# Loading the last DeltaNet pair into the gates' tile, and other banks and token orders for three blocks of an output projection

## The chip, the cores and the metric

The kernel runs on one core of a Trainium2 chip. The metric is the device time of one execution in microseconds. Engines are named as in the profile: PE is TensorE (matmuls; PEld its weight loads), DVE is VectorE, ACT is ScalarE, POOL is GpSimd, SP is SyncE, which here only issues DMAs. SPq, ACTq and POOLq are DMA issues on those engines' queues.

## The reference

One decoder layer for 512 tokens of width 2048, in fp32. Two causal token mixers work side by side on the normalised input, an mLSTM with 8 heads and a gated DeltaNet with 16 heads of 128 channels; their outputs go through one output projection each, are merged with sigmoid gates and added to the residual.

```python
u = _rmsnorm(h, norm_w)
proj = jnp.matmul(u, w_in)                    # 2048 x 20528, split into q, k, v, gates, ...
...
h_a = _mlstm_chunkwise(...)                   # then norm, sigmoid and silu gates
...
qkv = _causal_conv_silu(dn_qkv, dn_conv_w)    # four taps and silu on q, k, v of DeltaNet
...
h_b = _gated_delta_chunkwise(dq, dk_, dv_, beta, g)
h_b = _merge_heads(_rmsnorm(h_b, dn_norm_w)) * jax.nn.silu(dn_z)

y_a = jnp.matmul(h_a, w_out[:ML_WIDTH])
y_b = jnp.matmul(h_b, w_out[ML_WIDTH:])
return jax.nn.sigmoid(gate_a) * y_a + jax.nn.sigmoid(gate_b) * y_b
```

The result is `h + y`, and a last RMSNorm goes over it.

## The kernel before

Each fp32 operand of a big matmul is split into two parts of a faster format, hi and lo, and three products are added (hi x hi, hi x lo, lo x hi). For weights, `split_hi` is a cast on ACT (L135, `wh<-wr`) and `split_lo` a subtraction on DVE (L138, `wl<-wr,wh`). Weight tiles come through a ring: `wr` (raw, four buffers, loaded by SP), `wh` and `wl` (four buffers each). Of the activations, `uh` and `ul` are the two parts, made on ACT (L1189) and DVE (L1190) from raw tiles `hr`.

The kernel runs in stages. First come the input projections. Then DeltaNet heads are done in pairs (`dn_unit`; eight pairs, the last is pair 7 with heads 14 and 15), with the mLSTM heads beside them. Each `dn_unit` projects k, v and q of its pair into two PSUM banks, and `conv_silu` takes them out: a copy to `yp` on ACT (L770), a multiplication with the last tap on ACT (L771), three taps on DVE (L773). Behind the projections the mixers go on: a triangular solve on DVE (`xi`, L889 and L891), whose result travels over DRAM (`xd`, `tt`) and comes back as `tn` (L907), small matmuls, a chain per head that collects the output in a bank `po`, and at last `gz` (L1040), which empties that bank. The head's output is transposed and written to `h_d` by four DMAs on ACT's queue.

While the last pair's mixer is still at work, the output projection of the mLSTM branch begins: three *wide blocks* (`wide_block`) of 512 output columns, called blocks 0, 1 and 2. Each has 16 rows of weights (row k is `kt` = k), and for each row four token tiles of 128 tokens (token 0 to 3, `c` in the code), three matmuls of 512 columns each: 192 matmuls. The rows 14 and 15 (`KTAIL`) are done together at the end, token by token, and behind each token `put_y` multiplies the block's result with its gate tile (`tgy`, in block 2 a quarter of the tile `X`) and adds it to `y_d` in DRAM (L1338, L1339). Each token has a PSUM bank of its own, from one of three pools: `pj` (3 banks), `wk` (3) and `o` (2); the `po` of the two heads of a pair are the two `o` banks.

Behind block 2 comes `seven_stage`, a fast matrix scheme with seven products in place of eight, for the DeltaNet branch. It needs, for each of the eight pairs, sums and differences of the two heads' outputs in split form (`h_pair`: four sums on DVE, L1248 to L1251, the split `tu` on ACT and DVE, and a write of the changed raw tile to `he_d`), and all sixteen outputs as `uh` and `ul` (`load_h2`, which reads `he_d` and `h_d` into four buffers `hs`, tiles named `hr`). It also prepares its own weights: three tiles `wr3` at a time, their differences `t13` (L528, L529), split like the others and with the same rings. The profile leaves off the numbers at the end of a name, so it prints `wr3` as `wr` and `t13` as `t`.

These three, `h_last` (the pair 7), `load_h2` and the first weights of `seven_stage` (`lead`), run beside block 2. Their pool `sb` takes the room of the mixers' pool `wk`, so it opens only when the mixers' last tile there is free (`close`).

PE's order is that of the program: the generators that are started run at a `tick` between matmuls. The other engines' orders are set by a scheduler at build time, by priorities (`urgent(level)`) and dependencies (`behind`: no earlier than the newest split on that engine). Each engine, and each engine's DMA queue, then works strictly in its order.

Of the kernel before, what the change touches and what calls it, by code (L numbers as in the profile page):

```python
# [8 lines left out]
F32 = mybir.dt.float32  # L9
# [6 lines left out]
P = 128  # L16
S = 512
NC = S // P
D = 2048
KT = D // P  # L20
NB = 256
KP = 2
NO = 512
# [4 lines left out]
YDRAIN = 2  # L28
# [4 lines left out]
KTAIL = 2  # L33
# [22 lines left out]
def hybrid_body(  # L56
# [152 lines left out]
    def urgent(level=1):  # L209
        return tc.high_priority(offset=level * PRIO)  # L210
# [33 lines left out]
    psj = pss.enter_context(tc.tile_pool(name="psj", bufs=3, space=PSUM))  # L244
    psw = pss.enter_context(tc.tile_pool(name="psw", bufs=3, space=PSUM))
    pso = pss.enter_context(tc.tile_pool(name="pso", bufs=2, space=PSUM))

    banks = (((psj, "pj"),) * 3 + ((psw, "wk"),), ((psw, "wk"),) * 2 + ((pso, "o"),) * 2)

    def proj_cm(col0, before=None, kind="i"):  # L250
        ps = [psj.tile([P, S], F32, tag="pj", name="pj") for _ in range(2)]
# [511 lines left out]
    def bc(col, n):  # L763
        return col.unsqueeze(2).to_broadcast([P, NC, n])

    def conv_silu(ps, ct, dst, level=1):
        yp = yps[cnt["yp"] % NYP]
        cnt["yp"] += 1
        with urgent(level):
            A.copy(yp[:, 3:S + 3], ps)  # L770
            A.mul(dst, yp[:, 3:S + 3], convc[:, 144 + ct:145 + ct])  # L771
        for j in (2, 1, 0):
            V.scalar_tensor_tensor(out=dst, in0=yp[:, j:j + S], scalar=convc[:, 48 * j + ct:48 * j + ct + 1], in1=dst,  # L773
                                   op0=ALU.mult, op1=ALU.add)
# [268 lines left out]
    def dn_unit(p, mh):  # L1043
        hs = (2 * p, 2 * p + 1)
# [27 lines left out]
            start(load_h(), 2, "B")  # L1072
        ps = proj_cm(DN_Q + dcol)
        u["qn"] = []
        for j in range(2):
            conv_silu(ps[j], hs[j], kq[j][:, 1, :], 3 if last else 1)
            qn = wp.tile([P, NC, P], F32, tag="tg", name="qn", bufs=3)
            u["qn"].append(qn)
            start(silu_end(kq[j][:, 1, :], (kq[j][:, 1, :], qn)), 4 + 3 * j, front)
# [148 lines left out]

    def h_raw(i):
        if i == KH - 1:  # L1230
            raw = [late["sb"].tile([P, S], F32, tag="hs", name="hs", bufs=4) for _ in range(2)]
        elif i % 2:
            raw = [wk.tile([P, S], F32, tag="rb", name="hs", bufs=3) for _ in range(2)]
        else:
            pair = wk.tile([P, 2, S], F32, tag="ls", name="hs", bufs=1)
            raw = [pair[:, n, :] for n in range(2)]
        with behind("S"):
            for n in range(2):
                load_tile(raw[n], h_d[2 * i + n])
        return raw  # L1240
# [29 lines left out]

    def h_last():

        yield 5
        raw = h_raw(KH - 1)
        yield 5
        yield from h_pair(KH - 1, raw)
# [42 lines left out]
    def wide_w(col, kt):  # L1319
        return [w[:, 0, :] for w in next_w("o", col, kt)]  # L1320

    def wide_block(nb, pools, place, then=()):

        sl = slice(nb * NO, (nb + 1) * NO)
        ps = [pool.tile([P, NO], F32, tag=t, name="py") for pool, t in pools]
# [22 lines left out]
        for gen, wait in then:  # L1348
            start(gen, wait)
        ks = range(KT)  # L1350
        for kt in ks[:KT - KTAIL]:
            w = wide_w(nb * NO, kt)
            for c in range(NC):
                products(ps, kt, c, *w, ks)
                if c % 2:
                    tick()
            if nb < YDRAIN:
                close()
        ws = [(kt, wide_w(nb * NO, kt)) for kt in ks[KT - KTAIL:]]
        for c in range(NC):  # L1360
            for kt, w in ws:
                products(ps, kt, c, *w, ks)
            tick()
            if c in tgs:
                with urgent(3):
                    put_y(c)
            else:
                start(put_last(), 1)
# [2 lines left out]
             wk.tile([P, NO], F32, tag="rb", name="tgy", bufs=3) if c == 2 else wp.tile([P, NO], F32, tag="tg", name="tgy", bufs=3),  # L1371
             lambda c: wp.tile([P, NO], F32, tag="tg", name="tgy", bufs=3))
    for b in range(YDRAIN):
        wide_block(b, ((psj, "pj"), (psw, "wk"), (psj, "pj"), (psj, "pj")), DRAIN[b])
    while "sb" not in late:
        tick()
        close()
# [238 lines left out]
                    tick()  # L1616
            done_c(c)

    wide_block(YDRAIN, banks[1], lambda c: X2[:, c // 2, c % 2, :], [(load_h2(), 1), (lead(), 18)])
    for b, blk in enumerate(OUTS):  # L1620
        seven(2 * KH * b, *blk)
    last_block()
# [33 lines left out]
```

## Time and profile before

| | |
|---|---|
| median of 3 runs | 2229.91 us (2222.15 to 2234.51) |
| the profiled execution | 2228.3 us |
| its span in the profile | 2226.5 us |
| PE, DVE, ACT, POOL busy | 2157.8, 1650.0, 1022.2, 265.2 us |
| DMA, mean over the span | 196 GB/s |
| DMA from 1950 to 2010 us | 271 GB/s |

A timeline row has the start in us, the duration in us, the engine, the line of the kernel, the operation and `out<-in`, the number of rows merged into it (`x3`), and in brackets how long the engine was idle before it and what ended that. Matmuls are pipelined: a matmul's duration of 0.39 us is longer than the distance to the next one, so the time that a wait costs is read from the distance of the starts. Block 0 starts at 1846.95 us of the span, block 2 at 1951.2, `seven_stage` at 2005.69.

### The profile page before, as it was taken

The numbers are of one execution on the slowest core, as the hardware profiler recorded it, in microseconds if no ns is written. First come the engines' busy times: TensorE is split into PE (matmuls) and PEld (weight loads), VectorE is DVE, ScalarE is ACT, GpSimd is POOL, SyncE is SP. The second block draws the span as 40 slices with busy tenths as digits, with TensorE's granted clock in tenths as the row PEclk, the third lists the DMA queues.
The fourth block names the chain that finished last, engine by engine and source line by source line (L and its number), as shares of the span: only waits on it lengthen the run. The fifth ranks groups of instructions, "written<-read, shape, count | busy, mean of one in ns | idle before, by whom it ended". The sixth has DMA issues, their size and how long they took to land. (4 is left out here: it accounts for less than half of the span.)

```text
span 2226.5 us, 31649 instructions
## 1 busy us (share of the span) xinstructions
PE 2157.8 (97%) x10592; PEld 1770.6 (80%) x10592; DVE 1650.0 (74%) x2883; ACT 1022.2 (46%) x1986; POOL 265.2 (12%) x356
## 2 busy tenths in 40 slices
PE   6999999999999999999999999999999999989997
PEld 5877878888788788888888788888787887867775
DVE  5787788788778777877597786757575777567776
ACT  5444444445444444444545544444444454334344
POOL 0320000000000000000222412212122211110101
PEclk9999999999999999999999999999999999999999
DMA  5456666667667766776776767767666668695896
GB/s 156 124 176 197 196 202 198 209 200 234 192 211 232 236 197 215 231 241 190 198 201 165 172 161 174 165 160 172 161 145 162 152 157 230 176 268 184 247 323 220
DMA packets 534821, 435.81 MB, mean 196 GB/s; under 512 B 241921, under 2 KB 393698, under 8 KB 534530
## 3 DMA queue, kind: packets, MB, share of 16 engines
q1 hardware_dynamic: 425058, 357.68, 56.3%
q10 hardware_dynamic: 105568, 68.77, 9.7%
q0 software_dynamic: 4032, 7.34, 2.2%
q8 instruction: 83, 1.36, 0.2%
q14 instruction: 80, 0.66, 0.1%
HBM read 342.37 MB, written 95.49 MB: 197 GB/s over the span
## 5 line engine op out<-in xcount | busy, mean ns | idle before, releaser
L135 ACT CAST wh<-wr 128x512 fp32r<-128x512 f32 (+1 forms) x538 | 379.2, 706 | 416.3 <-PE pj L262 229.3
L138 DVE TENSOR_TENSOR wl<-wr,wh 128x512 fp32r<-128x512 f32 (+1 forms) x538 | 440.9, 822 | 152.9 <-ACT wh L135 142.7
L261 PE MATMUL pj<-uh,wh 128*128 128x512 f32 x1024 | 428.6, 419 | 0.0
L263 PE MATMUL pj<-uh,wl 128*128 128x512 f32 x1024 | 402.6, 393 | 0.0
L262 PE MATMUL pj<-ul,wh 128*128 128x512 f32 x1024 | 402.1, 393 | 0.0
L576 PE MATMUL ps<-wl,uh 128*128 128x512 f32 x704 | 277.7, 394 | 6.7 <-DVE wl L138 6.5
L575 PE MATMUL ps<-wh,uh 128*128 128x512 f32 x704 | 276.1, 392 | 6.3 <-DVE X L617 6.0
L577 PE MATMUL ps<-wh,ul 128*128 128x512 f32 x704 | 274.9, 391 | 0.0
L135 ACT CAST wh<-ts 128x512 fp32r<-128x512 f32 x224 | 138.2, 617 | 258.2 <-DVE ts L535 199.7
L135 ACT CAST wh<-t 128x1024 fp32r<-128x1024 f32 x112 | 117.8, 1052 | 250.0 <-PE ps L577 129.2
L263 PEld LDWEIGHTS pj<-uh,wl 128*128 128x128 f32 x1024 | 193.4, 189 | 42.6
L576 PE MATMUL ps<-wl,suh 128*128 128x512 f32 x576 | 224.3, 389 | 1.7 <-DVE wl L138 1.7
L575 PE MATMUL ps<-wh,suh 128*128 128x512 f32 x576 | 224.4, 390 | 0.6 <-ACT wh L135 0.3
L577 PE MATMUL ps<-wh,sul 128*128 128x512 f32 x576 | 224.1, 389 | 0.0
L261 PEld LDWEIGHTS pj<-uh,wh 128*128 128x128 f32 x1024 | 194.3, 190 | 35.2
L262 PEld LDWEIGHTS pj<-ul,wh 128*128 128x128 f32 x1024 | 194.3, 190 | 32.9
L138 DVE TENSOR_TENSOR wl<-ts,wh 128x512 fp32r<-128x512 f32 x224 | 153.7, 690 | 38.5 <-ACT wh L135 38.5
L138 DVE TENSOR_TENSOR wl<-t,wh 128x1024 fp32r<-128x1024 f32 x112 | 137.7, 1229 | 47.5 <-ACT wh L135 46.6
L576 PEld LDWEIGHTS ps<-wl,uh 128*128 128x128 f32 x704 | 132.3, 188 | 43.6 <-DVE wl L138 17.3
L575 PEld LDWEIGHTS ps<-wh,uh 128*128 128x128 f32 x704 | 132.3, 188 | 40.1 <-DVE X L617 12.4
L577 PEld LDWEIGHTS ps<-wh,ul 128*128 128x128 f32 x704 | 132.5, 188 | 26.6
L535 DVE TENSOR_TENSOR ts<-wr 128x512 f32<-128x512 f32 x112 | 77.3, 690 | 102.8 <-DMA wr<-t_d 77.0
(302 smaller groups left out, 3475.6 us busy)
## 6 DMA issues: line engine op xcount, KB each, us to landing
wr<-in_w_in_dram SPq DMA_DIRECT2D x704, 256.0 KB, 3.7
wr<-in_w_out_dram SPq DMA_DIRECT2D x138, 256.0 KB, 5.1
t_d<-ts ACTq DMA_DIRECT2D x96, 256.0 KB, 4.0
wr<-t_d SPq DMA_DIRECT2D x96, 256.0 KB, 4.0
wr<-in_w_in_dram SPq DMA_DIRECT2D x64, 128.0 KB, 3.4
xt<-in_x_dram SPq DMA_DIRECT2D x8, 512.0 KB, 7.3
tg_d<-X ACTq DMA_DIRECT2D x16, 256.0 KB, 6.1
tg_d<-to ACTq DMA_DIRECT2D x16, 256.0 KB, 5.7
```

Source lines behind the costliest of these rows:

```text
L135: newest["A"] = A.copy(hi, src).ins
L138: newest["V"] = V.tensor_tensor(out=lo, in0=src, in1=hi.bitcast(F32), op=ALU.subtract).ins
L261: T.matmul(ps[j], hi[:, k, wsl], uh[:, kt, :], start=(kt == 0), stop=False)
L262: T.matmul(ps[j], hi[:, k, wsl], ul[:, kt, :], start=False, stop=False)
L263: T.matmul(ps[j], lo[:, k, wsl], uh[:, kt, :], start=False, stop=(kt == KT - 1))
L535: V.tensor_tensor(out=ts[:, 0, :], in0=r[:, 0, :], in1=r[:, 2, :], op=ALU.subtract)
L575: T.matmul(ps[t], ah, hi, start=(g == "A" and i == 0), stop=False, skip_group_check=True)
L576: T.matmul(ps[t], ah, lo, start=False, stop=False, skip_group_check=True)
L577: T.matmul(ps[t], al, hi, start=False, stop=(i == KH - 1), skip_group_check=True)
```

## The change

There are four edits.

1. In the last pair's q projection, both banks are copied to `yp` first, at high priority, and the multiplications follow at normal priority (`conv_in`).
2. Block 0 begins with rows 0 and 1 of tokens 0 and 1, then rows 0 and 1 of tokens 2 and 3 (`behind_=2`); from row 2 on the order is as before. The ticks keep their number.
3. The raw tiles of pair 7 go to half 0 of the gates' tile `X` (where the gates of tokens 0 and 1 come later) in place of two of the four `hs` buffers, and `h_last` loads them at once instead of five ticks later.
4. Block 2 takes the banks wk, wk, o, pj in place of wk, wk, o, o, and ends in the token order 2, 0, 1, 3.

```diff
-    banks = (((psj, "pj"),) * 3 + ((psw, "wk"),), ((psw, "wk"),) * 2 + ((pso, "o"),) * 2)
+    JB, WB, OB = (psj, "pj"), (psw, "wk"), (pso, "o")
...
-    def conv_silu(ps, ct, dst, level=1):
+    def conv_in(ps, level=1):
         yp = yps[cnt["yp"] % NYP]
         cnt["yp"] += 1
         with urgent(level):
             A.copy(yp[:, 3:S + 3], ps)
+        return yp
+
+    def conv_silu(ps, ct, dst, level=1, yp=None):
+        if yp is None:
+            yp = conv_in(ps, level)
+        with urgent(level):
             A.mul(dst, yp[:, 3:S + 3], convc[:, 144 + ct:145 + ct])
...
         u["qn"] = []
+        yq = [conv_in(ps[j], 3) for j in range(2)] if last else (None, None)
         for j in range(2):
-            conv_silu(ps[j], hs[j], kq[j][:, 1, :], 3 if last else 1)
+            conv_silu(ps[j], hs[j], kq[j][:, 1, :], yp=yq[j])
...
         if i == KH - 1:
-            raw = [late["sb"].tile([P, S], F32, tag="hs", name="hs", bufs=4) for _ in range(2)]
+            raw = [late["X"][:, 0, n, :] for n in range(2)]
...
     def h_last():
 
-        yield 5
         raw = h_raw(KH - 1)
...
-    def wide_block(nb, pools, place, then=()):
+    def wide_block(nb, pools, place, then=(), behind_=0, ending=range(NC)):
...
-        for kt in ks[:KT - KTAIL]:
-            w = wide_w(nb * NO, kt)
-            for c in range(NC):
-                products(ps, kt, c, *w, ks)
-                if c % 2:
-                    tick()
-            if nb < YDRAIN:
+        ws = {}
+        order = [(kt, c) for c in (0, 2) for kt in range(behind_) ] + [(kt, c) for kt in ks[behind_:KT - KTAIL] for c in (0, 2)]
+        for n, (kt, c0) in enumerate(order):
+            if c0 == 0:
+                ws[kt] = wide_w(nb * NO, kt)
+            for c in (c0, c0 + 1):
+                products(ps, kt, c, *ws[kt], ks)
+            tick()
+            if n % 2 and nb < YDRAIN:
                 close()
...
-        for c in range(NC):
+        for c in ending:
...
-        wide_block(b, ((psj, "pj"), (psw, "wk"), (psj, "pj"), (psj, "pj")), DRAIN[b])
+        wide_block(b, (JB, WB, JB, JB), DRAIN[b], behind_=0 if b else 2)
...
-    wide_block(YDRAIN, banks[1], lambda c: X2[:, c // 2, c % 2, :], [(load_h2(), 1), (lead(), 18)])
+    wide_block(YDRAIN, (WB, WB, OB, JB), lambda c: X2[:, c // 2, c % 2, :], [(load_h2(), 1), (lead(), 18)], ending=(2, 0, 1, 3))
```

What this does to the engines' orders is shown at three places. First PE at the start of block 0; `py_18034` to `py_18037` are the banks of tokens 0 to 3, `wh_17908` and `wh_17945` the hi parts of rows 0 and 1. Before:

```order
L1317 MATMUL py_18034<-wh_17908,ul_88 128x512
L1315 MATMUL py_18035<-wh_17908,uh_87 128x512
L1316 MATMUL py_18035<-wl_17909,uh_87 128x512
L1317 MATMUL py_18035<-wh_17908,ul_88 128x512
L1315 MATMUL py_18036<-wh_17908,uh_87 128x512
L1316 MATMUL py_18036<-wl_17909,uh_87 128x512
```

After:

```order
L1323 MATMUL py_18035<-wh_17908,ul_88 128x512
L1321 MATMUL py_18034<-wh_17945,uh_87 128x512
L1322 MATMUL py_18034<-wl_17946,uh_87 128x512
L1323 MATMUL py_18034<-wh_17945,ul_88 128x512
L1321 MATMUL py_18035<-wh_17945,uh_87 128x512
L1322 MATMUL py_18035<-wl_17946,uh_87 128x512
L1323 MATMUL py_18035<-wh_17945,ul_88 128x512
L1321 MATMUL py_18036<-wh_17908,uh_87 128x512
```

Six matmuls of row 1 stand ahead of token 2's first one. ACT at the same place has moved the second copy (`yp1`) ahead of the first multiplication; the `h_d` write between the copies stays.

The second place is DVE in the middle of block 2; `wl_19187` is row 8 before and `wl_19215` row 9, `wl_19194` and `wl_19216` are these rows after. Before:

```order
L138 TENSOR_TENSOR wl_19165<-wr_19140,wh_19164 128x512
L528 TENSOR_TENSOR t13_19364<-wr3_19285 128x1024
L529 TENSOR_TENSOR ts_19363<-wr3_19285,t13_19364 128x512
L138 TENSOR_TENSOR wl_19187<-wr_19162,wh_19186 128x512
L138 TENSOR_TENSOR wl_19377<-t13_19364,wh_19376 128x1024
L528 TENSOR_TENSOR t13_19455<-wr3_19311 128x1024
L138 TENSOR_TENSOR wl_19215<-wr_19184,wh_19214 128x512
```

After:

```order
L138 TENSOR_TENSOR wl_19172<-wr_19144,wh_19171 128x512
L138 TENSOR_TENSOR wl_19194<-wr_19169,wh_19193 128x512
L528 TENSOR_TENSOR t13_19362<-wr3_19283 128x1024
L529 TENSOR_TENSOR ts_19361<-wr3_19283,t13_19362 128x512
L138 TENSOR_TENSOR wl_19375<-t13_19362,wh_19374 128x1024
L138 TENSOR_TENSOR wl_19216<-wr_19191,wh_19215 128x512
L528 TENSOR_TENSOR t13_19453<-wr3_19309 128x1024
```

Row 8's split has moved ahead of the first `t13`; row 9's stands behind the split of `t13` now and no longer behind the second `t13`. On ACT row 5's cast has moved in the same way, between the second and the third of the last four `h_d` writes, which stood together.

The third place is ACT near the end of block 2; `wh_19343` and `wh_19380` are rows 14 and 15 before, `wh_19315`, `wh_19341` and `wh_19378` rows 13, 14 and 15 after, `tu` the last pair's split. Before:

```order
L135 CAST wh_19343<-wr_19315 128x512
L1189 ACTIVATE tu_19196<-hsum_19197,normc_82 128x768
L135 CAST wh_19367<-ts_19363 128x512
L1189 ACTIVATE uh_87<-hr_19136,normc_82 128x512
L1254 DMA he_d_18033<-hs_19132 128x512
L1189 ACTIVATE uh_87<-hr_19158,normc_82 128x512
L135 CAST wh_19372<-wr3_19285 128x512
L1189 ACTIVATE uh_87<-hr_19180,normc_82 128x512
L135 CAST wh_19380<-wr_19341 128x512
```

After:

```order
L1196 ACTIVATE tu_19134<-hsum_19135,normc_82 128x768
L135 CAST wh_19315<-wr_19287 128x512
L531 DMA t2o_d_19057<-ts_19501 128x512
L1261 DMA he_d_18033<-X2_19056 128x512
L135 CAST wh_19341<-wr_19313 128x512
L1196 ACTIVATE uh_87<-hr_19112,normc_82 128x512
L1196 ACTIVATE uh_87<-hr_19140,normc_82 128x512
L135 CAST wh_19365<-ts_19361 128x512
L1196 ACTIVATE uh_87<-hr_19165,normc_82 128x512
L135 CAST wh_19370<-wr3_19283 128x512
L1196 ACTIVATE uh_87<-hr_19187,normc_82 128x512
L135 CAST wh_19378<-wr_19339 128x512
```

`tu` and the `he_d` write have moved from behind row 14's cast to ahead of it; between the casts of rows 14 and 15 stand four `uh` instead of three and `tu`.

On SP's queue the two raw loads of pair 7 (`X2<-h_d`) stand directly ahead of the first `hr` load, where they stood behind five of them, three weight loads and the gate loads, and the four gate loads of block 2, which stood together, are now two (tokens 2 and 3), one and one (tokens 1 and 0, the last behind the `he_d` write). In block 0, two of the four `hs` loads that stood ahead of the `xd` writes have moved behind them.

## The prediction

> **What bounds the kernel now.** I read the page first (busy time by engine), then the list of waits of TensorE, then the timeline at each wait that touches the changed lines, and the busy time and DMA share of the stage there.
>
> ```profile
> span 2226.5 us, 31649 instructions
> PE 2157.8 (97%) x10592; PEld 1770.6 (80%) x10592; DVE 1650.0 (74%) x2883; ACT 1022.2 (46%) x1986; POOL 265.2 (12%) x356
> ```
>
> TensorE is busy 97% of the span, and the change leaves it the same matmuls. So all that can be won is idle time of TensorE, and only that near the three wide blocks (blocks 0, 1, 2 below; block 0 starts at 1846.95 us, block 2 ends at 2005.7). These are the waits of TensorE, first for 1846 to 1952 us and then, from the second line, for 1950 to 2012 us (total, times, longest):
>
> ```profile
> PE py L1315 <- ACT yp L770: 2.2, 2, 1.8
> ...
> PE py L1315 <- ACT wh L135: 4.3, 1, 4.3
> PE py L1315 <- DVE gz L1040: 2.1, 1, 2.1
> PE py L1316 <- DVE wl L138: 1.3, 3, 0.5
> PE ps L575 <- DVE X L1338: 1.0, 1, 1.0
> ```
>
> They sum to 10.9 us, and each has a line in the diff near it. Block 2 is the dear one:
>
> ```profile
> 1951.20:2005.70 54.50, 46.88 (x194) 36.81 (x193) 36.14 (x53) 20.96 (x33) 5.00 (x7) 0.97 0.95 277
> ```
>
> Matmuls that do not wait start 0.227 us apart (five steps from 1846.95 to 1848.09 in the next fence), so its 192 matmuls need 43.6 us of these 54.5: 10.9 us are lost, some of it at a granted clock below one (0.97), with the DMA engines 95% busy.
>
> **Start of block 0.** Both accumulators of the last projection must be copied out by ScalarE (yp) before tokens 2 and 3 get a bank:
>
> ```profile
> 1846.95 0.39 PE L1315 MATMUL py<-wh,uh 128*128 128x512 f32 x1
> ...
> 1848.09 0.39 PE L1317 MATMUL py<-wh,ul 128*128 128x512 f32 x1
> 1850.29 0.50 PE L1315 MATMUL py<-wh,uh 128*128 128x512 f32 x1 [1.81 <-ACT yp L770]
> ...
> 1850.86 0.39 PE L1317 MATMUL py<-wh,ul 128*128 128x512 f32 x1
> 1851.62 0.50 PE L1315 MATMUL py<-wh,uh 128*128 128x512 f32 x1 [0.37 <-ACT yp L770]
> ...
> 1849.65 0.59 ACT L770 COPY yp<-pj 128x512 f32<-128x512 f32 x1 [1.45 <-DVE xi L891]
> ...
> 1851.01 0.56 ACT L770 COPY yp<-pj 128x512 f32<-128x512 f32 x1
> ```
>
> Lost: 2.20-0.23 before the first, 0.76-0.23 before the second, and 0.11 of slower pitch behind each (0.34 instead of 0.23): 2.7 us. With the lag, twelve matmuls stand ahead of token 2 instead of six, which ends at 1846.95+12x0.227=1849.67. The first copy ends at 1850.24, so 0.6+0.1 us stay. The second copy no longer waits for the multiply and ends near 1850.9, when token 3 comes up (1850.29+3x0.227=1850.97): no wait. The row-1 weights are needed 1.4 us earlier; I cost that at nothing, since TensorE took row 1 straight behind row 0 here with no wait. **Gain 2.0 us.** The multiplies come about 1 us later, at lower urgency; the first products with q stand 6 weight rows behind, and DVE is the cover there.
>
> What is late next is the triangular solve of the last DeltaNet pair, whose result tn TensorE takes in row 14 of block 0:
>
> ```profile
> 1878.85 2.15 SPq L1186 DMA_DIRECT2D hs<-h_d  x4
> 1880.58 0.17 DVE L891 TENSOR_TENSOR xi<-xi,tmp 128x8 f32<-128x8 f32 x1
> 1882.25 2.52 SPq L903 DMA_DIRECT2D xd<-xi  x4
> ...
> 1890.57 0.45 DVE L907 STREAM_TRANSPOSE tn<-tt 128x256 f32<-128x256 f32 x1 [4.33 <-DMA tt<-xd]
> 1891.16 0.69 PE L945 MATMUL p<-tn,aq 32*32 32x32 f32 x32
> ```
>
> tn is ready at 1891.02 and used at 1891.16: slack 0.14 us. TensorE would arrive 2.0 us sooner, while the solve's chain is DVE and DMA, not TensorE. In the new order of SP's queue, two of the four hs loads (2.15 us) go behind the xd writes, so xd can start about 1.1 us sooner (at most 1.5: xi was done at 1880.75). So 2.0-1.1=**0.9 us are given back** (bounds 0 and 2.0; I take the value from the half of the hs row).
>
> **Head of block 2.** Token 3 waits for the accumulator of the last head:
>
> ```profile
> 1953.02 0.39 PE L1317 MATMUL py<-wh,ul 128*128 128x512 f32 x1
> 1954.65 0.68 DVE L1040 TENSOR_TENSOR gz<-po,gz 128x512 f32<-128x512 f32 x1
> 1955.48 0.47 PE L1315 MATMUL py<-wh,uh 128*128 128x512 f32 x1 [2.07 <-DVE gz L1040]
> ```
>
> 2.46-0.23 plus 0.07 of slower pitch: 2.3 us. Token 3 now takes a pj bank, which block 1 leaves early; token 2 takes the o bank that was no wait here. **Gain 2.3 us.**
>
> **Middle of block 2.** The pair's difference t13 of the next stage (printed t) sits in VectorE's queue among the splits of the block's weights, and its three tiles wr3 (printed wr) can be loaded only when the mixers' pool is free:
>
> ```profile
> 1967.65 1.28 SPq L505 DMA_DIRECT2D wr<-in_w_out_dram  x3
> ...
> 1973.60 1.23 DVE L528 TENSOR_TENSOR t<-wr 128x1024 f32<-128x1024 f32 x1 [7.58 <-DMA wr<-in_w_out_dram]
> ...
> 1974.90 1.05 ACT L135 CAST wh<-t 128x1024 fp32r<-128x1024 f32 x1 [6.93 <-DVE t L528]
> ...
> 1976.07 1.22 DVE L138 TENSOR_TENSOR wl<-t,wh 128x1024 fp32r<-128x1024 f32 x1
> ...
> 1976.20 0.50 PE L1316 MATMUL py<-wl,uh 128*128 128x512 f32 x1 [0.52 <-DVE wl L138]
> ...
> 1985.32 0.50 PE L1316 MATMUL py<-wl,uh 128*128 128x512 f32 x1 [0.36 <-DVE wl L138]
> ```
>
> Lost before, by the longer pitch: 0.7 at row 8, 0.5 at row 12, 0.1 between: 1.3 us. After, row 8's split stands ahead of t13 and is safe, but row 9's stands behind it and behind the whole split of t13. Nothing in the change frees the pool sooner, so t13 still starts near 1973.6 on this clock: t13 1.23, ScalarE's 1.05 and the wl of 1.22 one behind the other, then row 9's 0.68 gives 1977.8. TensorE, 2.3+0.7 us sooner, wants row 9 at 1951.2+108x0.227=1975.7. So it waits 2.1 there. Rows 12 and 13 now have the last pair's sums and tu ahead of them on VectorE: about 1 us, an estimate by the 0.94 that tu takes on ScalarE (next fence). So **3.1 instead of 1.3: 1.8 us lost** (bounds: 0 if the loads land 2 us sooner, 4 if two later).
>
> **Tail of block 2.** The 4.3 us wait is for row 15's cast:
>
> ```profile
> 1984.16 1.03 SPq L1186 DMA_DIRECT2D hs<-h_d  x2
> ...
> 1992.73 0.94 ACT L1189 ACTIVATE tu<-hsum,normc 128x768 fp32r<-128x768 f32 x1 [2.17 <-DVE hsum L1249]
> ...
> 1997.23 0.72 ACT L1189 ACTIVATE uh<-hr,normc 128x512 fp32r<-128x512 f32 x1 [1.27 <-DMA hr<-h_d]
> 1997.86 0.60 ACT L135 CAST wh<-wr 128x512 fp32r<-128x512 f32 x1
> ...
> 1993.18 0.37 SPq L1186 DMA_DIRECT2D hr<-h_d  x1
> ...
> 1993.83 0.39 PE L1317 MATMUL py<-wh,ul 128*128 128x512 f32 x1
> 1998.51 0.50 PE L1315 MATMUL py<-wh,uh 128*128 128x512 f32 x1 [4.30 <-ACT wh L135]
> 1999.39 0.70 PE L1316 MATMUL py<-wl,uh 128*128 128x512 f32 x1 [0.38 <-DVE wl L138]
> ...
> 2002.88 0.43 PE L1315 MATMUL py<-wh,uh 128*128 128x512 f32 x1
> ```
>
> Lost: 4.45 up to 1998.51, 0.65 up to 1999.39, and 3.49 us for eight matmuls that need 1.81: 6.8 us. On ScalarE tu waited for the raw pair, loaded at 1984.16 into two of the four hs buffers, so that only two were left for the hr tiles; the last uh ahead of the cast waited for an hr issued as late as 1993.18. Now the pair's step moves as a whole: its two loads on SP ahead of the first hr (they stood behind five hr, four gate and three weight loads), its four sums and tu on VectorE and its tu and he_d write on ScalarE ahead of the casts of rows 13 and 14; POOL gets nothing. From the cast of row 14 to that of row 15 ScalarE has four uh (0.72) and two casts (0.60), 4.1 us; the last hr takes the buffer of the one that is split right ahead of tu, so it can be issued near 1989 (row 13 is wanted at 1951.2+156x0.227+3=1989.6), lands 4.05 us later as the one of 1993.18 did, and 1.23 behind that (1997.23 to 1998.46) the cast ends: 1994.3. TensorE wants row 15 at 1951.2+171x0.227+3.1=1993.1: a wait of 1.2, and 0.6 for wl. The stretch of slow matmuls followed the wait of 4.3 and none followed those of 1.81 and 2.07, so I take it as gone. **Gain 6.8-1.8=5.0 us** (bounds: 0 if the hr lands no sooner, 6.3 if only wl is late).
>
> The Trainium skill, "TensorE: Matmul & The Clock Gate", section "HAM oscillation", puts the limit for such a stretch at an idle gap of about 3.4 us. By it a wait of 3 us at row 15 would still be free of the slow stretch and the sum would be 1.2 us worse than mine, while by the rows alone it might also pay 1.7 on top; the rows fit the page but do not reach between 2.07 and 4.3.
>
> **Hand-over to the next stage.** Its first product needs both o banks:
>
> ```profile
> 2007.56 0.50 PE L575 MATMUL ps<-wh,tu 128*128 128x512 f32 x1 [1.02 <-DVE X L1338]
> ```
>
> About 1.3 us with 0.3 of pitch, as at the waits above. Token 2 now ends first, and only it holds an o bank, freed 18 matmuls (4 us) before the block ends: **gain 1.3 us**. The new wait on SP is token 0's gate, which must follow the he_d write of the raw pair, with the next hr and wr3 loads queued behind it; he_d leaves some 5 us sooner than before, and these loads serve matmuls that stand 5 us or more behind, so I cost it at nothing. Without that cover it is rival 3.
>
> **Sum:** 2.0-0.9+2.3-1.8+5.0+1.3=7.9 us. The profiled run took 2228.3 us (span 2226.5 and 1.8 around it), 1.6 below the median 2229.9 of the runs. So I expect 2220.4 in its place, and 2222 as a median.
>
> **Rivals.** One row of the list of DMA issues from 1950 to 2010 us is needed (count, size, us from issue to landing):
>
> ```profile
> hs<-h_d SPq DMA_DIRECT2D x2, 256.0 KB, 6.1
> ```
>
> (1) *Bytes decide.* Block 2 runs at 95% DMA share, and the change moves loads without removing one. If the last hr ahead of row 15's cast lands no sooner than 1997.2, block 2 ends as before, only block 0's 1.1 and the hand-over's 1.3 stay: 2227. For it: the 95%. Against it: the last hr was issued at 1993.18 because of buffers, not bytes. The Trainium skill, "DMA: Bandwidth & Descriptors", section "Issuing engines are not separate DMA queues", says that all issuing engines share the same 16 DMA engines, which speaks for this rival. (2) *All of it goes*: tn and the hr tiles come in time, nothing at row 9: 2.7+10.9+1.3=14.9 us, 2215. Against it: t13 ahead of row 9. (3) *Slower.* Row 5's cast now stands between the last h_d writes on ScalarE, whose landing, with he_d, frees the pool for wr3; every us that it adds is paid once at row 9, and token 0's gate is a second load with a late source. If the last three writes each wait for a full landing as the hs loads did (6.1 us) instead of overlapping, wr3 comes 18 us late and the time is 2222+18=2240. It beats my gain from 8 us on.
>
> **Chances.** Forecast 0.58, with its own range 2217 to 2227 (the bounds of the terms and 3 us for the runs, which spread from 2222.15 to 2234.51); rival 1 0.25; rival 2 0.11; rival 3 0.06. From 2214 to 2231 all but rival 3 and the outer runs are held. A change of 0.5% is 11.1 us, about what a measurement of this kernel can tell from none: faster than 2218.8 are rival 2 and a seventh of the forecast, 0.19; slower than 2241 is half of rival 3 with a stray run, 0.05; the rest 0.76.
>
> **What the profile after would show.** Block 0: one wait for yp below 1 us, and a new wait for tn at the first 32x32 products. Block 2: no wait for gz; a wait of 1 to 3 us for wl or wh at row 9; row 15 below 2.5 us, with a granted clock of 1.0 throughout; no wait for X at the next stage's first product; DMA share still above 0.9. I am wrong if row 9 waits over 5 us, or row 15 as long as before, or if a wait appears at the next stage on the put of token 0.

## The result and the profile after

The changed kernel takes 2219.24 us (median of 14 executions, 2212.04 to 2221.84), the kernel before 2228.68 (14 executions, 2222.15 to 2234.51). The ratio is 0.9956 with a 95% interval of 0.9947 to 0.9966: 9.4 us faster, 0.44%. The forecast was 2222 as a median, from a sum of 7.9 us.

From the page of the changed kernel, the span and TensorE's row:

```profile
span 2214.5 us, 31648 instructions
PE 2153.4 (97%) x10592; PEld 1767.4 (80%) x10592; DVE 1648.3 (74%) x2883; ACT 1023.1 (46%) x1986; POOL 264.2 (12%) x356
```

This span is 12.0 us below that of before, and 4.5 of them lie ahead of the change: block 0 starts at 1842.41 us where it started at 1846.95, though no engine's order differs up to there. So the traces are compared from block 0 on, in three stretches: block 0 to the start of block 2, block 2, and the rest. Busy time by stretch: behind the length stand the busy times of PE, PEld, DVE, ACT and POOL, each with its number of instructions, then the granted clock, the DMA share and the GB/s. First the changed kernel:

```profile
1842.41:1944.56 102.15, 101.77 (x581) 84.21 (x580) 70.31 (x160) 41.38 (x96) 14.06 (x18) 1.00 0.73 200
1944.56:1996.05 51.49, 46.27 (x194) 37.05 (x192) 35.29 (x52) 21.00 (x33) 4.68 (x7) 0.97 0.97 289
1996.05:2214.50 218.45, 200.97 (x865) 160.63 (x863) 162.78 (x224) 96.62 (x153) 18.18 (x22) 0.98 0.80 247
```

And before, the first and the last of the three:

```profile
1846.95:1951.20 104.25, 102.06 (x581) 84.25 (x580) 70.82 (x160) 41.15 (x95) 14.28 (x18) 1.00 0.72 195
...
2005.69:2226.50 220.81, 201.17 (x865) 160.54 (x863) 162.99 (x224) 96.15 (x153) 18.01 (x22) 0.98 0.78 243
```

The first stretch gave 2.1 us, block 2 (54.49 before) 3.0, the rest 2.4: 7.5 us in this pair of profiles. A second profile of each kernel gives 106.39, 54.99 and 222.78 before and 103.81, 50.49 and 217.78 after; over both pairs the three stretches gave 2.3, 3.8 and 3.7, which is 9.8 us and fits the 9.4 of the medians.

TensorE's waits in the changed kernel from 1840 to 2010 us (total, times, longest):

```profile
PE py L1321 <- ACT wh L135: 4.0, 2, 2.0
PE py L1322 <- DVE wl L138: 1.2, 2, 0.8
PE py L1321 <- ACT yp L770: 0.4, 1, 0.4
```

gz and X no longer stand there, and the wait for tn that was forecast does not appear. The two waits for wh are rows 9 and 15 of block 2. Row 9 in the timeline:

```profile
1968.31 1.23 DVE L528 TENSOR_TENSOR t<-wr 128x1024 f32<-128x1024 f32 x1 [8.60 <-DMA wr<-in_w_out_dram]
...
1969.62 1.04 ACT L135 CAST wh<-t 128x1024 fp32r<-128x1024 f32 x1 [10.63 <-DMA wr<-in_w_out_dram]
1970.57 0.61 ACT L135 CAST wh<-wr 128x512 fp32r<-128x512 f32 x1
...
1971.23 0.50 PE L1321 MATMUL py<-wh,uh 128*128 128x512 f32 x1 [2.03 <-ACT wh L135]
...
1971.84 0.68 DVE L138 TENSOR_TENSOR wl<-wr,wh 128x512 fp32r<-128x512 f32 x1
...
1972.58 0.50 PE L1322 MATMUL py<-wl,uh 128*128 128x512 f32 x1 [0.84 <-DVE wl L138]
```

VectorE was idle for 8.6 us ahead of t13, whose load was not there, and ScalarE for 10.6 ahead of the cast of t13; row 9's split and cast stand behind these. Row 15:

```profile
1987.75 0.72 ACT L1196 ACTIVATE uh<-hr,normc 128x512 fp32r<-128x512 f32 x1 [2.63 <-DMA hr<-he_d]
...
1989.23 0.72 ACT L1196 ACTIVATE uh<-hr,normc 128x512 fp32r<-128x512 f32 x1 [0.25 <-DMA hr<-h_d]
...
1989.86 0.60 ACT L135 CAST wh<-wr 128x512 fp32r<-128x512 f32 x1
...
1990.52 0.50 PE L1321 MATMUL py<-wh,uh 128*128 128x512 f32 x1 [1.97 <-ACT wh L135]
...
1991.40 0.50 PE L1322 MATMUL py<-wl,uh 128*128 128x512 f32 x1 [0.38 <-DVE wl L138]
```

The cast still stands behind uh splits whose hr tiles are late, 2 us now and not 4.3.

### The profile page after: what moved, and what is told of

It reads as the page before. It is cut to its first block, busy times and chain, and to the rows that moved or that the text cites. A ratio compares the mean times of both kernels' runs of the same rounds, so it can differ in the third digit from the quotient of the medians.

```text
span 2214.5 us, 31648 instructions
## 1 busy us (share of the span) xinstructions
PE 2153.4 (97%) x10592; PEld 1767.4 (80%) x10592; DVE 1648.3 (74%) x2883; ACT 1023.1 (46%) x1986; POOL 264.2 (12%) x356
## 4 chain that ended last, share of the span: by engine, by line
PE 72%; DMA 12%; DVE 8%; issue 3%; SPq 2%; ACT 1%; POOL 1%; DVEq 0%; ACTq 0%; POOLq 0%
PE ps L576 12%; PE ps L577 11%; PE ps L575 11%; PE pj L261 9%; PE pj L262 9%; PE pj L263 9%; DVE wl L138 3%; DMA wr<-t_d 3%; DMA wr<-in_w_in_dram 2%; PE py L1321 2%; PE py L1323 2%; PE py L1322 2%; ACT wh L135 1%; DMA hmr<-hm_d 1%; DMA wr<-in_w_out_dram 1%
## 5 line engine op out<-in xcount | busy, mean ns | idle before, releaser
L138 DVE TENSOR_TENSOR wl<-t,wh 128x1024 fp32r<-128x1024 f32 x112 | 137.1, 1224 | 48.0 <-ACT wh L135 47.3
L575 PEld LDWEIGHTS ps<-wh,uh 128*128 128x128 f32 x704 | 132.1, 188 | 38.3 <-DVE X L617 10.6
```

The source lines that it names most:

```text
L138: newest["V"] = V.tensor_tensor(out=lo, in0=src, in1=hi.bitcast(F32), op=ALU.subtract).ins
L575: T.matmul(ps[t], ah, hi, start=(g == "A" and i == 0), stop=False, skip_group_check=True)
```

## The experiments

Each run was profiled. The stretches are those above, in us; a ratio is to the kernel before, run on the same chip in the same rounds, with its 95% interval. Kernels without one ran once.

| kernel | median us | ratio | block 0 to 2 | block 2 | rest |
|---|---|---|---|---|---|
| before | 2228.68 | 1 | 104.25 | 54.49 | 220.81 |
| before, again | 2231.11 | | 106.39 | 54.99 | 222.78 |
| changed | 2219.24 | 0.9956 (0.9947 to 0.9966) | 102.15 | 51.49 | 218.45 |
| changed, again | 2216.48 | | 103.81 | 50.49 | 217.78 |
| edits 1 and 2 alone | 2225.11 | 0.9983 (0.9971 to 0.9996) | 102.99 | 54.89 | 222.82 |
| edit 4 alone | 2226.03 | 0.9987 (0.9974 to 1.0000) | 105.87 | 52.58 | 221.01 |
| edit 3 alone | 2227.09 | 0.9993 (0.9982 to 1.0004) | 105.77 | 52.17 | 224.75 |
| changed, row 9 ahead of t13 | 2219.08 | 0.9957 (0.9944 to 0.9971) | 102.36 | 51.16 | 219.73 |
| the same, load_h2 late | 2220.97 | 0.9968 (0.9956 to 0.9979) | 102.55 | 47.59 | 225.79 |
| the same, wr3 triples late | 2227.34 | 1.0001 (0.9988 to 1.0014) | 104.05 | 59.33 | 219.75 |
| changed, raw pair late | 2224.79 | | 102.44 | 48.22 | 224.68 |
| changed, ending 0, 1, 2, 3 | 2218.40 | | 102.02 | 52.13 | 217.79 |
| five moves in block 2 | 2215.35 | 0.9943 (0.9926 to 0.9959) | 102.91 | 47.27 | 221.54 |
| the same, again | 2216.61 | 0.9948 (0.9935 to 0.9961) | 102.84 | 46.98 | 219.53 |

**One edit at a time.** Edit 4 alone, on the kernel before:

```diff
-    wide_block(YDRAIN, banks[1], ..., [(load_h2(), 1), (lead(), 18)])
+    wide_block(YDRAIN, (WB, WB, OB, JB), ..., [(load_h2(), 1), (lead(), 18)], ending=(2, 0, 1, 3))
```

> The kernel before with edit 4 alone (block 2's banks wk, wk, o, pj and its end in the order 2, 0, 1, 3). Two theories. Order: each wait is set by what stands ahead in one engine's queue. Then the wait for gz at the head (2.3 us) and the wait for X at the hand-over (1.3) go, row 9's split is now behind the first t13 on VectorE and waits about 2 us, and row 15 keeps its time on the clock, because the raw pair still sits in the hs buffers: its wait grows from 4.3 to about 5 and block 2 stays at 54 to 55 us; only the hand-over is kept, 1 to 2 us in all. Bytes: block 2's end is set by the transfers and also stays at 54.5. What tells this run is whether edit 4 by itself moves row 8's split ahead of t13 and whether its 2.3 us survive: if block 2 falls to 52 us, both theories are wrong about row 15.

Waits of TensorE in block 2's middle, from its timeline:

```profile
1973.25 0.50 PE L1322 MATMUL py<-wh,uh 128*128 128x512 f32 x1 [1.50 <-ACT wh L135]
1974.59 0.50 PE L1323 MATMUL py<-wl,uh 128*128 128x512 f32 x1 [0.84 <-DVE wl L138]
```

gz and X do not wait any more, and row 9 does, as expected: so it is the banks' edit that moves row 8's split ahead of t13. But row 15 did not keep its time; it waited 2.9 in place of 4.3 and block 2 came down to 52.58. Neither theory had that.

Edit 3 alone (the raw pair in X, at once):

```diff
-            raw = [late["sb"].tile([P, S], F32, tag="hs", name="hs", bufs=4) for _ in range(2)]
+            raw = [late["X"][:, 0, n, :] for n in range(2)]
...
-        yield 5
         raw = h_raw(KH - 1)
```

> The kernel before with edit 3 alone (the raw pair in half 0 of X, loaded at once). Order: row 15's wait of 4.3 us and the slow stretch behind it (6.8 us with the wait for wl) shrink to 2 to 3 us, block 2 takes 50 to 51.5 us in place of 54.5, the waits for gz (2.1) and X (1.0) stay, and the kernel is 3 to 4.5 us faster. Bytes: the DMA share stays at 0.95 and the end of block 2 with it: 54 us or more, no change in time.

The one wait for wh in its list of waits is row 15's:

```profile
PE py L1321 <- ACT wh L135: 2.3, 1, 2.3
```

4.3 became 2.3, as the order theory has it. Block 2 got 2.3 us shorter than the first profile of before (52.2 us, still 0.7 above the expected bound) and moved the same 15 MB, the GB/s times the length: so bytes alone do not set its end. The rest got longer by 2.0 to 3.9 us, and the time is only 1.5 us down, less than I expected. Part of it in this profile is the clock (below): it has periods at half clock at 1850.66, 1956.47 and 2052.05 us, behind waits for yp, gz and a later X, that the first profile of before does not have. What the edit itself costs in the rest, this run cannot say.

Edits 1 and 2 alone (`conv_in`, `behind_=2` in block 0):

> The kernel before with edits 1 and 2 alone (both yp copies first, rows 0 and 1 of tokens 2 and 3 behind those of tokens 0 and 1). Block 0 and block 1 together take 102.2 us in place of 104.3 (one wait for yp of 0.3 to 0.8, none for tn). Order theory: the first t13 is ready at a time set by the mixers and the loads, so row 8's split, which stands behind it, comes at most 0.8 sooner while TensorE comes 2.1 sooner: block 2 takes 55 to 56 in place of 54.5, and 0.5 to 1.5 us stay. Clock theory (a period of 3.41 us in which TensorE is idle for more than half is followed by one at half clock): the wait for yp of before costs a further 1.7 us in some executions and the short one never, so the median falls by about 1 us more than the rows of one profile say: 2 to 3 us in all, near 2226. If the parts added up, this one would have to give 5.4 us, what is left of 9.4 after 2.5 and 1.5.

The first stretch fell to 102.99 and block 2 rose to 54.89, both within a microsecond of the forecast, and the ratio says 3.8 us (0.9 to 6.5). That holds the 2 to 3 us with the clock and also the upper part of the 0.5 to 1.5 without it, so this run does not settle between the two. The three parts give 1.7 + 1.3 + 0.7 thousandths, 3.7 together against 4.4 for the whole, with intervals of over one thousandth each: they add up within what was measured.

**What holds row 9.** The changed kernel with the first t13 and its splits held behind row 9's (`mark` is set three rows earlier, when row 9's cast and split are the newest):

```diff
+                if kt == 9 - SAHEAD:
+                    mark.update({e: newest[e] for e in "VA"})
...
-            prep_sums(0)
-            prep_pair(0)
+            with ExitStack() as held_:
+                for e in mark:
+                    held_.enter_context(tc.issue_after(mark[e]))
+                prep_sums(0)
+                prep_pair(0)
```

> The changed kernel, but the first t13 of the next stage and its splits are held behind row 9's cast and split on ScalarE and VectorE. Order: row 9 no longer waits (3.3 us with its wl) and the slow stretch behind it (1.7) goes; row 10 waits at most 0.8. What becomes of the 5 us: (a) row 15's cast stands behind uh splits whose hr tiles are loaded at a time set by the pool's opening and four buffers, not by TensorE; then row 15 comes no sooner on the clock, its wait grows from 2.4 to 6 or 7 and block 2 stays near 51 us; (b) the hr tiles follow TensorE, and block 2 falls to 47 us. I expect (a), 0.7 to 0.3. If row 9 still waits, its wait was not for t13.

Row 9 no longer waits: its wait was for t13. The 5 us came back as (a) said, but not where. Row 15 did not grow; rows 11, 12, 13 and 15 wait for wl, four waits of 0.6 to 1.3 us:

```profile
PE py L1325 <- DVE wl L138: 4.0, 4, 1.3
```

and on VectorE the raw pair's sum stands in the place of t13 as an instruction whose load is late, with row 11's split behind it:

```profile
1978.15 0.43 DVE L1260 TENSOR_TENSOR hsum<-X 128x256 f32<-128x256 f32 x1 [2.30 <-DMA X<-h_d]
```

**Fewer uh ahead of row 15.** The same with `load_h2` started 16 ticks later:

> As the run with row 9 ahead of t13, and load_h2 starts 16 ticks later, so that only four uh splits (the first four buffers) stand ahead of row 15's cast instead of eight. Order: both waits of block 2 go, block 2 takes 44 to 46 us in place of 51.5, and the loads that are left come in the next stage, whose DMA share is 0.80: it may wait up to 2 us for uh. 4 to 7 us faster than the changed kernel, near 2213. Bytes: the loads of block 2 fall by four tiles of 256 KB, about 3 us at 290 GB/s; then block 2 falls by 3 us at most and the next stage grows by as much: no gain.

Block 2 fell to 47.59, short of the 44 to 46 of the order theory, and the next stage took all of it back, which is what the bytes theory had. Its DMA share of 0.99 decides nothing, since blocks of 50 to 52 us show the same. What the next stage waited for can be seen. VectorE, and the next stage's wait:

```profile
2002.32 0.75 DVE L1200 SCALAR_TENSOR_TENSOR ul<-hr,normc,uh 128x512 fp32r<-128x512 f32 x1 [2.43 <-ACT uh L1199]
2003.95 0.75 DVE L1200 SCALAR_TENSOR_TENSOR ul<-hr,normc,uh 128x512 fp32r<-128x512 f32 x1 [0.88 <-ACT uh L1199]
2004.62 0.68 DVE L1347 SCALAR_TENSOR_TENSOR X<-X,py 128x512 f32<-128x512 f32 x1
```

```profile
2005.35 0.79 PE L575 MATMUL ps<-wh,tu 128*128 128x512 f32 x1 [3.44 <-DVE X L1347]
```

The last token's multiplication, which frees its bank, stands behind two ul whose hr tiles now come late.

**Less to load ahead of the raw pair.** The row 9 kernel with the second and third `wr3` triples loaded behind row 15's raw weights:

```diff
+            load_quad()
+            yield 6
...
+            yield 2
+            for _ in range(2):
+                with behind("S"):
+                    load_quad()
+                yield 2
```

> The changed kernel with row 9 ahead of the first t13 and, in addition, the second and third wr3 triples of the next stage (six tiles, 1.5 MB) loaded behind row 15's weights instead of with the first triple. The bytes of block 2 and the next stage together are the same. Queue and bytes: rows 10 to 15 wait because the raw pair and the hr tiles are queued behind 2.3 MB of wr3; with 1.5 MB of it taken out of the way (4 us at 380 GB/s) the raw pair lands about 4 us sooner, the waits of rows 10 to 15 (1.0, 1.4, 1.7, 0.9, 1.7 us from start to start) fall to under 0.5 each and block 2 takes 44.5 to 46.5 us in place of 51.2. The next stage needs the second triple 5.4 us behind its start and may wait 0 to 2 us for it. 4 to 6 us faster than the changed kernel, near 2214. Order alone (the waits come from the order on VectorE, not from the landing): block 2 stays at 50 us or more.

A miss: 59.33 us. VectorE waited for the raw pair up to 25.1 us into block 2, where it had been 28.4 with row 9 alone moved, so the transfers did come sooner. But the second t13 stood ahead of row 15's cast, as the first had ahead of row 9's, and its load was now among the last:

```profile
1990.36 1.23 DVE L528 TENSOR_TENSOR t<-wr 128x1024 f32<-128x1024 f32 x1 [2.90 <-DMA wr<-in_w_out_dram]
...
1991.62 1.04 ACT L135 CAST wh<-t 128x1024 fp32r<-128x1024 f32 x1 [4.51 <-DVE t L528]
...
1995.05 0.60 ACT L135 CAST wh<-wr 128x512 fp32r<-128x512 f32 x1
```

Row 15 waited 5.7 us for this cast, and three periods at half clock lie behind it (1993.80 to 2004.04 us).

**The halves of edits 3 and 4.** The changed kernel with the raw pair loaded five ticks later again, but still into X:

> The changed kernel, but the raw pair is loaded five ticks later, as before; it still goes to X and not to the hs buffers. If the two hs buffers were what held row 15 up (four for the hr tiles instead of two), row 15 waits 2 to 2.5 us as in the changed kernel. If the earlier load was what counted, it waits 4 us or more and a stretch at half clock follows. I expect the first; row 9's wait stays at 1 to 3 us.

Block 2 took 48.22. Row 15:

```profile
1992.27 0.50 PE L1322 MATMUL py<-wh,uh 128*128 128x512 f32 x1 [0.95 <-ACT wh L135]
...
1993.68 0.50 PE L1323 MATMUL py<-wl,uh 128*128 128x512 f32 x1 [0.91 <-DVE wl L138]
```

The wait is below both expected values, and far from the 4 us of the second. So, as far as one profile shows it, the two hs buffers that edit 3 gave back are what helps row 15, and the earlier load is not: block 2 was 2 to 3 us shorter without it. But the rest was 6 to 7 us longer than in the changed kernel, with no wait at its first product. 1.8 of that are a wait for a t2o_d tile 48 us into the stage, which before has too and the changed kernel has not (below); the rest of it was not traced. For the whole kernel the earlier load may therefore pay.

The changed kernel with block 2 ending in the order 0, 1, 2, 3:

> The changed kernel, but block 2 ends in the token order 0, 1, 2, 3; the banks stay wk, wk, o, pj. No wait for gz at the head (the bank decides that). The o bank of token 2 is emptied six matmuls (1.4 us) before the block ends instead of 18 (4.1 us); its multiplication takes 0.68 and stands behind two others on VectorE, so the next stage's first products wait 0 to 1 us for X. If they wait 1.4 us as before the change, the order alone made the hand-over free; if they do not wait at all, the bank did.

No wait for X at the hand-over, and the rest takes 217.79 as with the new order: the bank made the hand-over free, and the ending order adds nothing that these runs show.

**A version with all of it.** First t13 behind row 9, triples 2 and 3 behind the raw weights of rows 14 and 15, second t13 behind row 15, the raw pair's sums 9 ticks later, `load_h2` 12 ticks later with a pause behind its sixth uh:

```diff
-            yield 5 if k == KT - KTAIL - 1 else 2
+            yield 10 if k == 5 else 2
...
-                prep_sums(n0 + n + 1)
-                prep_pair(n0 + n + 1)
+                with ExitStack() as held_:
+                    if mark and not n0 + n:
+                        held_.enter_context(behind("V"))
+                        held_.enter_context(behind("A"))
+                    prep_sums(n0 + n + 1)
+                    prep_pair(n0 + n + 1)
...
-    ..., [(load_h2(), 1), (lead(), 18)], ending=(2, 0, 1, 3))
+    ..., [(load_h2(), 13), (lead(), 18)], ending=(2, 0, 1, 3))
```

> The changed kernel with five moves in block 2: the first t13 behind row 9; the second and third wr3 triples behind the raw weights of rows 14 and 15; the second t13 and its splits behind row 15's; the raw pair's sums 9 ticks later; load_h2 12 ticks later, with a pause behind its sixth uh, so that six uh stand ahead of row 15's cast and none of the others is late. What failed in the last run was the second t13, whose late load held up row 15's cast on ScalarE (5.7 us): that is gone here. Queue theory: rows 9 to 15 wait under 3 us together, block 2 takes 44.5 to 47.5 us in place of 50.5 to 51.5, and the next stage 218 to 221, as in the changed kernel: 3 to 6 us faster than it, 2213 to 2216. Rival (given back): as in the run with four late uh, the stage behind loses what block 2 gains, by a put or a uh that is late: the sum of both stays at 269 to 273 us and the time at 2218 to 2221.

The three stretches of its first profile:

```profile
1842.88:1945.79 102.91, 101.75 (x582) 84.20 (x581) 70.38 (x160) 41.77 (x96) 14.19 (x18) 1.00 0.74 199
1945.79:1993.06 47.27, 44.70 (x194) 35.88 (x193) 29.02 (x44) 18.96 (x30) 4.01 (x6) 1.00 1.00 290
1993.06:2214.60 221.54, 202.32 (x865) 160.25 (x863) 168.07 (x233) 97.69 (x156) 18.84 (x23) 0.98 0.82 248
```

Block 2 runs at a granted clock of 1.00 throughout and at a DMA share of 1.00, and takes 47.3 us. The rest takes back 1 to 4.

> The kernel with the five moves in block 2 once more, for more executions of it: six gave 2215.35 us (0.9926 to 0.9959 of before) where the changed kernel has 0.9947 to 0.9966. If block 2's 3.7 us are kept, the ratio comes to 0.993 to 0.995 again; if the next stage takes them back, as the profile of the first run says of 3.4 us of them, it comes to 0.9955 or 0.996, like the changed kernel. Rows: 102 to 104 us from block 0 to block 2, block 2 at 46 to 48, the rest at 219 to 222.

0.9948 (0.9935 to 0.9961), and 0.9943 the first time. Both lie below the changed kernel's 0.9956, but the intervals overlap: by the ratios it is 2 to 3 us faster than the changed kernel, which these runs do not settle.

**The clock.** The two kernels as they are, profiled again:

> The kernel before, profiled once more, for the clock. Clock theory: every stretch at half clock begins one period of 3.41 us behind a period of the same grid in which TensorE was busy for less than half; the number of them ahead of block 0 differs between executions and accounts for the start of block 0 to within 1 us (1.7 us each). Row 15's wait of 4.3 us is followed by one in each execution, the waits for yp and gz (1.8 and 2.1) in some. Rival: the clock is lowered by the length of a single wait (over 2.3 us, say): then the waits for yp and gz are never followed by one.

> The changed kernel, profiled once more. Row 9 waits 2.0 and 0.8 us again and has a stretch at half clock behind it (idle for 2.3 of 3.41 us); row 15 waits 2.0 and 0.4 and has one in about half of the executions. From block 0 to block 2: 102.2 us; block 2: 51.5, or 53.2 with both stretches.

The changed kernel did not repeat itself at row 9: there the second profile has one wait of 0.65 us, for wl, and no stretch at half clock. Row 15 has one (below).

In all 14 profiles the stretches at half clock (slow periods from here on), but for the last one at the end of the span, last 3.41 us or a multiple, and those of one profile lie on one grid: in the changed kernel they begin at 1683.01 and 1973.15 us, 85 times 3.413 apart. The next rows cut the span into these periods. Before, around the wait for yp, where no period is busy for less than half:

```profile
1845.92:1849.34 3.42, 2.56 (x12) 1.78 (x10) 3.42 (x9) 1.96 (x3) 0.00 (x0) 1.00 1.09 314
1849.34:1852.75 3.41, 2.09 (x8) 1.44 (x9) 2.32 (x9) 2.46 (x5) 0.00 (x0) 1.00 1.16 296
1852.75:1856.16 3.41, 3.41 (x17) 2.82 (x16) 3.41 (x8) 3.41 (x7) 0.00 (x0) 1.00 1.14 292
```

Edit 3 alone, the same wait (1.83 and 0.36 us where it was 1.81 and 0.37), which falls into one period:

```profile
1847.25:1850.66 3.41, 1.22 (x5) 0.56 (x4) 2.59 (x7) 2.27 (x5) 0.00 (x0) 1.00 1.14 314
1850.66:1854.07 3.41, 3.41 (x8) 2.70 (x9) 3.41 (x9) 2.92 (x6) 0.00 (x0) 0.50 1.20 308
```

With 1.22 us of work in 3.41, the next period is granted 0.50: 17 matmuls become 8. Row 9 of the changed kernel is such a case too: 1.5 us of its wait of 2.03 and all of the 0.84 lie in one period:

```profile
1969.73:1973.15 3.42, 1.08 (x4) 0.67 (x5) 2.99 (x4) 2.07 (x3) 0.00 (x0) 1.00 1.08 370
1973.15:1976.56 3.41, 3.41 (x10) 2.67 (x9) 3.41 (x6) 1.56 (x2) 0.00 (x0) 0.50 1.09 376
```

Over the 14 profiles, from 100 to 2195 us, 33 periods had TensorE idle for 1.91 us or more, and all 33 were followed by one at half clock; of 37 with 1.60 to 1.91 it was 21, and of 60 with 1.20 to 1.60 it was 7. So the rival, a limit on the length of one wait, falls: what counts is how much of a period is idle, with the change-over mostly near half of it and no sharp edge. That every slow period follows one that is idle for more than half, as I expected, is not quite so. My expectation of the start of block 0 falls too: it lay at 1841.2 to 1847.7 us over the 14, and the slow periods ahead of it explain only some of that (two of them with 1841.24 in one run, two with 1847.42 in another).

## Why the prediction was right, and where it was off

**Start of block 0** (gain 2.0; 0.7 left): in the first pair as written, one wait from start to start of 0.77 in place of 2.20 and 0.76. It varies, though. In the second profile of the changed kernel the copy came 4.3 us into the block and not 2.6, since the two uh ahead of it on ScalarE wait for a load, and TensorE waited 2.1 us, more than the 1 us that I gave as a bound:

```profile
1843.77 1.60 ACT L1196 ACTIVATE uh<-hr,normc 128x512 fp32r<-128x512 f32 x2 [3.56 <-DMA hr<-hm_d]
...
1846.96 0.58 ACT L770 COPY yp<-pj 128x512 f32<-128x512 f32 x1 [1.08 <-DVE tmp L895]
...
1847.60 0.50 PE L1321 MATMUL py<-wh,uh 128*128 128x512 f32 x1 [2.10 <-ACT yp L770]
```

What the step left out is the clock. The old wait for yp brought a slow period in three of the four profiles that have it (before again, edit 3 alone, edit 4 alone), not in the one I read; the changed kernel's in neither. That is about 1.7 us more in three of these four profiles.

**tn** (0.9 given back): did not happen; this step failed. The changed kernel:

```profile
1874.53 0.18 DVE L897 TENSOR_TENSOR xi<-xi,tmp 128x8 f32<-128x8 f32 x1
1874.88 2.52 SPq L909 DMA_DIRECT2D xd<-xi  x4
...
1882.98 0.45 DVE L913 STREAM_TRANSPOSE tn<-tt 128x256 f32<-128x256 f32 x1 [3.32 <-DMA tt<-xd]
...
1884.52 0.69 PE L951 MATMUL p<-tn,aq 32*32 32x32 f32 x32
```

tn is ready at 1883.43 and used at 1884.52: 1.1 us of slack, where I had a wait; none of the 14 profiles has one. Counted from block 0, xd starts 2.8 us sooner (32.5 for 35.3) and not 1.1: 1.3 is the gap behind xi on SP (0.17 for 1.50), and 1.5 is the solve itself, which ends 32.3 us into block 0 for 33.8. The premise that failed is that the solve's chain is VectorE and DMA and does not follow TensorE. The second profile of before shows that it does: TensorE came to the products with tn 46.35 us into block 0 and not 44.21, the solve ended 2.2 us later too (36.0), and VectorE, with splits of the block's weights among the solve's steps, waited 2.2 us for their casts and not 0.7. I had also left VectorE's own queue as it was, though the multiplications that come later on ScalarE bring their taps later, behind steps of the solve; a wait of 1.0 us of VectorE for one of them is gone. How the 1.5 us divide between the two was not tested.

**Head of block 2** (gain 2.3): right. No kernel with the new banks waits for gz. Here too the clock is missing: the wait for gz brought a slow period in three of four profiles (before again, edits 1 and 2 alone, edit 3 alone).

**Middle** (3.1 left): the mechanism was right, as the row 9 run shows. The size is 2.42 + 1.34 - 0.45, 3.3 us, and 1.7 of slow clock in the first profile, all of it at row 9 and none at row 12, where I had put 1. In the second it is 1.03 + 1.30 - 0.45 = 1.9 us, of which 1.1 lies at row 12.

**Tail** (1.8 left): the term that was mis-sized. 2.36 + 0.88 - 0.45 = 2.8 us, and in the second profile 2.52 + 0.88 - 0.45 = 3.0 and a slow period. I took a landing of 4.05 us from one hr row; the hr that counted was issued 38.4 us into block 2, near the 37.8 that I had, and its uh started 6.3 us later:

```profile
1982.96 0.37 SPq L1193 DMA_DIRECT2D hr<-h_d  x1
```

The same trace of before has a median landing of 5.5 us for these loads (`hr<-h_d`, 1944 to 2010 us): my one row was one of the quicker ones. And I took the clock of 1.0 from single waits of up to 2.07 us. The same wait at row 15, first and second profile:

```profile
1986.80:1990.21 3.41, 1.75 (x8) 1.13 (x6) 1.77 (x4) 2.21 (x4) 0.00 (x0) 1.00 1.06 373
1990.21:1993.63 3.42, 2.73 (x11) 2.06 (x12) 2.89 (x5) 2.13 (x4) 0.00 (x0) 1.00 1.05 377
```

```profile
1986.84:1990.25 3.41, 1.28 (x7) 0.74 (x5) 2.54 (x4) 2.43 (x4) 0.00 (x0) 1.00 1.08 385
1990.25:1993.66 3.41, 3.25 (x7) 2.26 (x8) 2.82 (x5) 2.17 (x3) 0.17 (x1) 0.50 1.01 359
```

Block 2 gave 3.0 and 4.5 us in the two pairs, where the steps said 2.3 - 1.8 + 5.0 = 5.5.

**Hand-over** (gain 1.3): 1.41 - 0.23 = 1.2, right in size, wrong in cause: the ending order has no part in it. Token 0's gate cost nothing, as forecast. Missing is a wait 47 us into the next stage, 1.97 from start to start before and none after: a difference waited for its t2o_d tile. Before, and after:

```profile
2051.65 0.69 DVE L535 TENSOR_TENSOR ts<-wr 128x512 f32<-128x512 f32 x1 [2.36 <-DMA wr<-t2o_d]
```

```profile
2038.67 0.69 DVE L535 TENSOR_TENSOR ts<-wr 128x512 f32<-128x512 f32 x1 [1.43 <-DMA wr<-t2o_d]
```

It comes 42.6 us into the stage and not 46.0. Its tile was issued on SP 38.4 us into the stage and not 41.5, and took as long to land (4.1 and 4.3 us). Why SP came to it sooner the runs do not show. The hand-over and this wait are 3.2 us in the first pair and 3.0 in the second, of 2.4 and 5.0 for the whole stretch; what the rest of it did was not traced.

So 7.9 came near the 9.4 in part by luck, since errors of both signs cancel: the tail gave 1 to 3 us less than its term, tn 0.9 more, the next stage about 1.7 that was in no term, and each of two removed waits of about 2 us carried a slow period in three profiles of four, which the one trace I read had at neither place.

**Rivals.** Bytes do not decide: block 2 moved 15 MB, the GB/s times the length, in 54.5 us before and in 51.5 and 50.5 changed, and 14.6 MB took 52.6 us with edit 4 alone and 48.2 with the raw pair late. Nor is a DMA share near 1 a limit: single periods above show 1.06 to 1.20 and up to 385 GB/s, where block 2 as a whole has 273 to 305. Whether bytes hold it where it takes 47 to 48 us with loads moved into the next stage, these runs do not show. That all of it goes was excluded by rows 9 and 15. The slower rival, a triple 18 us late, did not come; t13 started 125.9 us behind block 0, 0.75 sooner than before.

## What to carry to other kernels

A cast or split that stands behind an instruction with a late load waits for that load, whatever its own data: ask of each strict queue which instruction stands ahead and when its load lands, and expect the next late one to take its place when you move it. A wait taken away pays only if the next wait on the same queue is not due by then; three of these runs freed 2 to 5 us in one place and lost them again in the next rows or the next stage. One profile is one throw of the clock: price a wait of about 2 us with the chance of a slow period, not with what followed it in the one trace at hand.

## What the hardware showed that I had not expected

TensorE's clock is decided in periods of 3.413 us on a grid that does not start with the waits. A period with 1.91 us or more of idle time was always followed by one at half clock (33 of 33), so a wait costs about 1.7 us more, half of a period, or nothing, by where it falls: the wait for gz was 2.07 us without a slow period in the first profile of before and 2.08 with one in the second. Two waits of 1.83 and 0.36 us in one period count together. The Trainium skill, "TensorE: Matmul & The Clock Gate", section "What's actually happening", has a free-running window of 3413 ns, which these traces agree with. The rule that the prediction took from the Trainium skill, "TensorE: Matmul & The Clock Gate", section "HAM oscillation", an idle gap of more than about 3.4 us, does not hold here: those waits of 1.83 and 0.36 us were enough.
